# A transformer block on one core: where weight sums are made, and first left sums without PSUM copies

## The chip, the cores and the metric

One Trainium2 chip, one of its cores. The metric is the device time of one execution in microseconds (us). The engines are PE (TensorE, matmuls), PEld (its weight loads), DVE (VectorE), ACT (ScalarE), POOL (GpSimd) and SP (SyncE, which here only issues DMAs). Each engine runs its own instructions in order; an instruction that waits holds up all behind it on its engine.

## The reference

One hybrid decoder block on a sequence of 2048 tokens with 1024 channels, all in float32:

```python
h = _rmsnorm(x, norm_pre_mix)
proj = h @ w_in
y_attn = _mixer_dilated_attention(q, k, v)
y_gmlp = _mixer_chunked_gmlp(u, z, ...)
merged = gate_a * (y_attn @ w_branch_attn) + gate_b * (y_gmlp @ w_branch_gmlp)
x = x + _rmsnorm(merged @ w_out, norm_post_mix)
h = _rmsnorm(x, norm_pre_mlp)
a = relu(h @ w_mlp_in)
x = x + _rmsnorm((a * a) @ w_mlp_out, norm_post_mlp)
```

## The kernel before

**Products.** Each float32 operand is split into a high part of type fp32r (`hi`, a converting copy, mostly on ACT) and the rest (`lo = src - f32(hi)`, a subtraction, mostly on DVE). A product is three matmuls: high by high, high by low, low by high (`mm3`, L98). A 128x512 float32 result fills one of PSUM's eight banks.

**Part 1** makes the projections, the attention and the gate values. The change doesn't touch it.

**Part 2** works on four chunks of 512 tokens, in the order 2, 3, 0, 1. For each, `merge` goes over eight tiles `dt` of 128 channels: two products with the branch weights `wb`, times the gates `g` (loaded by `load_gate` on SP, sigmoid on ACT), summed and split into `mg`. Then four `out_block`s of 128 tokens multiply `mg` by `w_out` (two halves of 24 matmuls), take the norm, add `x` (tile `xr`, one buffer, loaded on SP), store the sum to `x1_d`, and make the normed rows `y1` (L1269). A block's eight transposes (`pt`, L1274) come later on PE: `flush_older` puts those of block 0 in the middle of block 2, those of block 1 in the middle of block 3; the others come in the next merge, or, after the last chunk, in the MLP. `tt` holds the transposed rows on the way to `h2_d`.

`merge` and the blocks also carry *pieces*. The MLP's first product uses a seven-product scheme for 2x2 blocks (Strassen's, in Winograd's form), at two levels, and needs sums of its weights' and its rows' quarters. `w_piece(t)` loads a pair of weight tiles on SP into `trw` and `tqw` (one buffer each), makes four sums on DVE, and stores them with two DMAs on POOL's queue to `ws_d`; `t_piece` does so with rows of `h2_d`. A call of `next_piece` either loads a piece or makes the sums of the one loaded, so a piece needs two calls. `PIECE_AT` says behind which `dt` of which chunk a call stands; one more stands behind each `out_block` of the first three chunks. `W_EARLY` is the number of weight pieces made here; the other of the 16 are made in the MLP.

The order on ACT, DVE, POOL and SP in this part is made by a scheduler. PE's is the written one.

**PSUM in part 2**: four banks for products, and four, with the tag `aux`, that rotate: `junk` (the target of a square), `pt`, and the copies described next. A tile gets the bank of the fourth tile before it in the written order.

**The MLP** has a written order on all engines. Its first half runs 7 x 8 steps of seven products of six matmuls; `k` counts these products. A step needs the *left sums* `hs_n`: raw weights `hraw_n` (two buffers, `load_ha`), of which `combine` makes seven operands: four sums on POOL and three splits of 128x512, `sa`, `sb` and `sc`, made by `staged`. `staged` copies a sum to its high part and a second time to a PSUM bank, both on ACT; DVE later subtracts from that bank. The sets `hs_0` and `hs_1` are made in part 2, before block 2 of the last chunk; these banks are of the tag `aux`, in the order sa, sb, sc, sa, sb, sc, and the two tiles `pt` of block 0 follow them.

`later(k, f, ...)` puts `f` behind product `k`. For the weight sums that part 2 leaves, `w_load` issues four loads, `w_sum` makes one sum each (two on DVE, two on POOL), `w_store` issues four stores.

Of the kernel before, what the change touches and what calls it, by code (L numbers as in the profile page):

```python
# [11 lines left out]
AF = mybir.ActivationFunctionType  # L12
# [8 lines left out]
KT = 8  # L21
# [7 lines left out]
def f32(ap):  # L29
    return ap.bitcast(F32) if ap.dtype != F32 else ap  # L30
# [12 lines left out]
def block_kernel(ctx, tc, a, out):  # L43
    nc = tc.nc
    pe, act, dve, pool, sp = nc.tensor, nc.scalar, nc.vector, nc.gpsimd, nc.sync
    x = a["x"]

    def stack(es, name, bufs=1, side=None, space=None):
        kw = dict(name=name, bufs=bufs, reuse_waits="tile")
        if side:  # L50
            kw["side"] = side
        if space is not None:
            kw["space"] = space
        return es.enter_context(tc.tile_pool(**kw))
# [11 lines left out]
    def psum_aux(name):  # L66
        return ps.tile([P, 512], F32, name=name, tag=aux_tag, bufs=BANKS[aux_tag])

    BANKS, aux_tag = dict(aux=4, a=3, bc=3, s=2), "aux"
# [112 lines left out]
    def behind():  # L182

        es, t = ExitStack(), mybir.EngineType
        for e in (t.Activation, t.DVE, t.Pool, t.SP):
            es.enter_context(tc.issue_after(next(i for i in reversed(nc.cur_bb.bb.instructions) if i.engine == e)))
        return es
# [969 lines left out]
    def load_y(c, engs=(("act", "dve"),)):  # L1157
        cs = slice(c * 512, (c + 1) * 512)
        yt = [bot.tile([P, 2, 512], F32R, name=f"yt{c}{k}", tag=f"yt{k}") for k in range(6)]
        for k in range(6):  # L1160
            split_in(yt[k], ya_d[k, :, cs] if k < 2 else yg_d[k - 2, :, cs], None, *engs[k % len(engs)])
        return yt
# [17 lines left out]
    def load_gate(c, dt, wch):  # L1180
        if dt < KT and (c, dt, wch) not in gates:
            d = chunks.index(c) * KT + dt
            pl, tag = (gtp, f"gt{wch}") if c == 2 or d % (5 - 2 * wch) < 3 - wch else (gxp[0], f"gx{wch}")
            gt = pl.tile([P, 512], F32, name=f"g{wch}_{c}{dt}", tag=tag, bufs=3 - wch if pl is gtp else 2 - wch)
            sp.dma_start(gt, gate_d[wch * 8 + dt, :, c * 512:(c + 1) * 512])
            gates[c, dt, wch] = gt
# [104 lines left out]
    def t_piece(kk):  # L1291

        w, v = (ttp.tile([P, 2, 512], F32, name=f"{n}{kk}", tag=n, bufs=1) for n in ("tq", "tr"))
        for t, k in ((w, kk), (v, kk + 2)):
            sp.dma_start(t.rearrange("p c t -> p (c t)"), h2_d[:, k, HALF:])
        yield
        b11, b12, b21, b22 = w[:, 0], w[:, 1], v[:, 0], v[:, 1]
        dve.tensor_sub(b11, b12, b11)
        dve.tensor_sub(b12, b22, b12)
        pool.dma_start(t_d[:, kk, 0:2], w)  # L1300
        dve.tensor_sub(b22, b22, b11)
        dve.tensor_sub(b21, b21, b22)
        pool.dma_start(t_d[:, kk, 2:4], v)
        yield

    def w_piece(t):

        w, v = (ttp.tile([P, 2, 512], F32, name=f"{n}w{t}", tag=n, bufs=1) for n in ("tq", "tr"))
        for z, n in ((v, t + NF // 2), (w, t)):
            sp.dma_start(z.rearrange("p a c -> p (a c)"), a["w_mlp_in"][n].rearrange("p k c -> p (k c)"))  # L1310
        yield
        a11, a12, a21, a22 = w[:, 0], w[:, 1], v[:, 0], v[:, 1]
        q, f = divmod(t, 2)
        dve.tensor_add(a22, a21, a22)
        dve.tensor_sub(a21, a11, a21)
        pool.dma_start(ws_d[q][:, 2:4, f], v)
        dve.tensor_sub(a11, a22, a11)
        dve.tensor_sub(a12, a12, a11)
        pool.dma_start(ws_d[q][:, 0:2, f], w)
        yield  # L1320

    W_EARLY = 14
    pieces = deque([w_piece(t) for t in range(W_EARLY - 2)] + [t_piece(0), t_piece(1)] +
                   [w_piece(t) for t in range(W_EARLY - 2, W_EARLY)])
    piece = []
    PIECE_AT = {2: (3, 5, 7), 3: (0, 2, 4, 6, 7), 0: (1, 3, 5, 7), 1: range(KT)}

    def next_piece():
        with behind():
            if piece:  # L1330
                next(piece.pop(), None)
            elif pieces:
                piece.append(pieces.popleft())
                next(piece[0])

    def merge_pieces(c, dt):
        if dt in PIECE_AT[c]:
            next_piece()
# [4 lines left out]
    def bank(name, tag):  # L1343
        return ps.tile([P, 512], F32, name=name, tag=tag, bufs=BANKS[tag])
# [2 lines left out]

    def staged(name, src, hi, lo):

        while len(unread) > 1:  # L1350
            unread[0]()
        t = bank(name, "s") if aux_tag != "aux" else psum_aux(name)
        if len(src.shape) == 4:
            t = t.rearrange("p (k m c) -> p k m c", k=2, m=2)
        elif len(src.shape) == 3:
            t = t.rearrange("p (k c) -> p k c", k=2)
        act.activation(hi, src, AF.Copy)  # L1357
        act.activation(t, src, AF.Copy)

        def read():  # L1360
            if read in unread:
                unread.remove(read)
                dve.tensor_sub(lo, t, f32(hi))

        unread.append(read)
        return read
# [56 lines left out]
    def sum_ha(n):  # L1423
        w = hs_[n] = ring(n, f"hs_{n}", [P, 2, 7, 256])
        yield from combine(n, w, hraw_.pop(n))
# [3 lines left out]
    def first_op(j):  # L1429

        name = OPS[j]
        for kk in range(2):
            w = w2_[(0, kk), name] = spot()
            if name[0] == "T":
                src = t_d[:, kk, T_AT.index(name)]
            else:
                k, t0 = kk + 2 * (name[1] == "2"), HALF + 512 * (name[2] == "2")
                src = h2_d[:, k, t0:t0 + 512]
            sp.dma_start(f32(w[1]), src)

    def first_split(j, kk, lo_eng="dve"):
        hi, lo = w2_[(0, kk), OPS[j]]
        split(hi, lo, f32(lo), "act", lo_eng)
# [91 lines left out]
    def w_load(t):  # L1535

        outer_t["w", t] = [rx.tile([P, 512], F32, name=f"wt{t}{m}", tag="xs" if (t - W_EARLY) % 2 else "c1", bufs=4) for m in range(4)]
        for m, z in enumerate(outer_t["w", t]):
# [131 lines left out]
    for n, c in enumerate(chunks):  # L1670
        if n:
            mg = merge(c, yt, {0: flush, 2: flush}, lambda dt: merge_pieces(c, dt))
        for i in range(4):
            b = out_block(c, i, mg, flush_older)
            next(b)
            last.append(b)
            if n < 3:
                next_piece()
            if n < 3 and not i:
                yt = load_y(chunks[n + 1])  # L1680
                for dt, wch in ((0, 0), (0, 1), (1, 0), (1, 1), (2, 0), (2, 1), (3, 0), (4, 0)):
                    with behind():
                        load_gate(chunks[n + 1], dt, wch)
            if n == 3 and i == 1:
                e2r.close()
                egx.close()
                rx = stack(e3, "rx", 1, side="right")
                r4 = stack(e3, "r4", 1, side="right")
                for m in range(4):
                    w = r4.tile([P, 2, 512], F32R, name=f"spot{m}", tag=f"spot{m}")  # L1690
                    spots.append((w[:, 0], w[:, 1]))
                for m in range(2):
                    w = [gtp.tile([P, 512], F32R, name=f"spot{4 + m}{h}", tag=f"gt{m}", bufs=3 - m) for h in range(2)]
                    spots.append(w)
                first_op(0)
                load_ha(0)
                first_op(1)
                load_ha(1)
                first_op(2)
                for g in sum_ha(0):  # L1700
                    pass
                for j in range(2):
                    for kk in range(2):
                        first_split(j, kk)
                for g in sum_ha(1):
                    pass
                for kk in range(2):
                    first_split(2, kk)
# [57 lines left out]
    aux_tag = "bc"  # L1766
# [176 lines left out]
    for n in range(8):  # L1943
        t = 4 + 4 * n
        for f, d, args in ((outer_load, 0, ()), (outer_sum, 4, (0,)), (outer_sum, 6, (2,)), (outer_store, 9, ())):
            later(t + d, f, n, *args)
    for n in range(NF // 2 - W_EARLY):
        t = 38 + 5 * n
        for f, d, args in ((w_load, 0, ()), (w_sum, 4, (0,)), (w_sum, 5, (1,)), (w_sum, 6, (2,)), (w_sum, 7, (3,)),
                           (w_store, 9, ())):  # L1950
            later(t + d, f, W_EARLY + n, *args)
    for q in range(HQ):
        t = 7 * (5 * HQ + 4) + 19 * q // 2
# [4 lines left out]
    for k, (_, stage, n, i) in enumerate(yorder):  # L1958
# [40 lines left out]
        elif i in (3, ("p", 7)):  # L1999
# [10 lines left out]
            if stage and not more:  # L2010
                f = finish(n)
# [73 lines left out]
```

## Time and profile before

| what | value |
|---|---|
| median of 3 runs | 2620.88 us (2618.87 to 2622.3) |
| the profiled execution | 2623.96 us |
| its span, first to last instruction | 2622.3 us |
| mean granted TensorE clock | 0.991 of full |
| PE busy | 2551.4 us, 97% |
| DVE, ACT, POOL busy | 64%, 49%, 52% |
| part 2 | about 1025 to 1437 us |
| first half of the MLP | 1437 to 1993 us |

The span is that of the execution that was profiled, and the time of that execution is a little longer. PE is busy nearly always, so what another engine does shows only where PE waits for it, in a list of who waited for whom (engine, line, releaser; then us in total, times, longest) and in the timeline, where the wait ahead of an instruction stands in square brackets. In the timeline a row is: start, duration, engine, line, operation, output<-inputs, shape. In the groups by line it is: count | busy us, mean ns of one | idle us ahead. In rows by window it is: window and its length, PE, PEld, DVE, ACT, POOL busy (and count), granted clock, DMA share, GB/s.

### The profile page before, as it was taken

Reading aid. Unit: us, or ns where it says so; the run is one execution under the profiler, and the core shown is the slowest. Engines: PE = TensorE matmul, PEld = TensorE weight load, DVE = VectorE, ACT = ScalarE, POOL = GpSimd, SP = SyncE. Lnnn points to the kernel's source line nnn. Section 1 sums busy time; section 2 is a strip of 40 time slices with the busy share of each in tenths; the row PEclk is TensorE's granted clock in tenths of the full one; section 3 lists DMA queues with packets and bytes.
Section 4 is the critical chain, followed back from the end, with each engine's and each line's share of the span. In section 5 each row is a group of like instructions: output and inputs, shape, how many; then the busy total and the mean of one; then the engine's idle time right before and its main releaser. Section 6 shows DMA issues by size and latency. Waiting matters only on the chain. (4 is left out here: it accounts for less than half of the span.)

```text
span 2622.3 us, 36291 instructions
## 1 busy us (share of the span) xinstructions
PE 2551.4 (97%) x12122; PEld 2126.4 (81%) x12122; DVE 1687.3 (64%) x3077; ACT 1294.4 (49%) x2714; POOL 1361.8 (52%) x1377
## 2 busy tenths in 40 slices
PE   9999999999999999999997999999999999999998
PEld 8888888888888887787775778878877888888886
DVE  5676575435443456866665677778776777677767
ACT  5213211244445434554433664675456776666755
POOL 0363254274555544311112656776798677677634
PEclk9999999999999999999998999999999999999999
DMA  8879778989898899866765765347885221222235
GB/s 313 285 246 325 258 235 276 309 261 284 275 312 227 237 305 338 281 242 232 260 226 195 271 196 180 122 145 240 261 270 159 89 89 58 88 89 84 89 117 209
DMA packets 411565, 568.73 MB, mean 217 GB/s; under 512 B 58737, under 2 KB 247409, under 8 KB 410354
## 3 DMA queue, kind: packets, MB, share of 16 engines
q1 hardware_dynamic: 385008, 501.58, 58.8%
q0 software_dynamic: 16480, 58.21, 5.7%
q10 hardware_dynamic: 9890, 6.62, 0.8%
q8 instruction: 96, 1.57, 0.2%
q14 instruction: 91, 0.75, 0.1%
HBM read 362.16 MB, written 204.14 MB: 216 GB/s over the span
## 5 line engine op out<-in xcount | busy, mean ns | idle before, releaser
L1570 PE MATMUL ha<-spot,hs 128*128 128x512 f32 x1344 | 326.6, 391 | 8.7 <-DVE e L1584 2.7
L1880 PE MATMUL ya<-spot,s 128*128 128x512 f32 x1344 | 324.0, 389 | 1.7 <-DVE X_yt L1888 1.4
L1570 PEld LDWEIGHTS ha<-spot,hs 128*128 128x128 f32 x1344 | 252.2, 188 | 65.3 <-DVE e L1584 4.4
L1880 PEld LDWEIGHTS ya<-spot,s 128*128 128x128 f32 x1344 | 252.0, 188 | 55.2 <-DVE X_yt L1888 1.8
L1357 ACT ACTIVATE s<-sraw 128x512 fp32r<-128x512 f32 x168 | 105.3, 627 | 152.5 <-POOL sraw L1409 113.3
L1357 ACT ACTIVATE hs<-hraw 128x512 fp32r<-128x512 f32 x168 | 105.2, 626 | 137.4 <-POOL hraw L1409 108.8
L731 PE MATMUL g<-opA,spots 128*128 128x512 f32 x672 | 170.6, 398 | 1.8 <-DVE cv L763 1.8
L1880 PE MATMUL yc<-spot,s 128*128 128x512 f32 x672 | 170.5, 389 | 0.0
L1570 PE MATMUL hc<-spot,hs 128*128 128x512 f32 x672 | 170.5, 389 | 0.0
L731 PE MATMUL g<-opB,spots 128*128 128x512 f32 x648 | 164.0, 397 | 0.0
L99 PE MATMUL x<-hT_a,wq 128*128 128x512 f32 x384 | 149.7, 390 | 0.0
L100 PE MATMUL x<-hT_a,wq 128*128 128x512 f32 x384 | 149.4, 389 | 0.0
L101 PE MATMUL x<-hT_a,wq 128*128 128x512 f32 x384 | 149.4, 389 | 0.0
L74 ACT ACTIVATE hl<-r 128x512 fp32r<-128x512 f32 x48 | 30.4, 633 | 237.3 <-POOL r L332 89.0
L1570 PEld LDWEIGHTS hc<-spot,hs 128*128 128x128 f32 x672 | 126.1, 188 | 26.3
L1880 PEld LDWEIGHTS yc<-spot,s 128*128 128x128 f32 x672 | 126.1, 188 | 26.2
L731 PEld LDWEIGHTS g<-opA,spots 128*128 128x128 f32 x672 | 121.0, 188 | 23.9 <-issue 2.2
L82 POOL TENSOR_TENSOR spots<-gr,spots 128x512 fp32r<-128x512 f32 x98 | 128.6, 1316 | 21.2 <-ACT spots L74 7.1
L1741 ACT ACTIVATE sraw<-sraw 128x1024 f32<-128x1024 f32 x128 | 134.7, 1053 | 1.7
L731 PEld LDWEIGHTS g<-opB,spots 128*128 128x128 f32 x648 | 116.9, 188 | 21.1
L82 POOL TENSOR_TENSOR spot<-w2r,spot 128x512 fp32r<-128x512 f32 x79 | 101.0, 1306 | 50.2 <-ACT spot L74 50.2
L76 POOL TENSOR_SCALAR spots<-gr 128x512 fp32r<-128x512 f32 x86 | 55.5, 645 | 132.8 <-PE g L731 91.4
(465 smaller groups left out, 6772.9 us busy)
## 6 DMA issues: line engine op xcount, KB each, us to landing
sraw<-sd SPq DMA_DIRECT2D x128, 256.0 KB, 3.3
qk<-hl SPq DMA_DIRECT2D x24, 1024.0 KB, 5.6
qq<-qk SPq DMA_DIRECT2D x96, 256.0 KB, 5.3
sd<-e SPq DMA_DIRECT2D x64, 256.0 KB, 4.6
hraw<-wsd SPq DMA_DIRECT2D x32, 512.0 KB, 4.7
w2r<-in_w_mlp_out_dram SPq DMA_DIRECT2D x16, 1024.0 KB, 8.4
g<-gated SPq DMA_DIRECT2D x56, 256.0 KB, 6.1
gr<-sgd SPq DMA_DIRECT2D x53, 256.0 KB, 5.0
```

The lines of the kernel that those rows point to most:

```text
L74: act.activation(hi, src, AF.Copy)
L76: pool.tensor_scalar(hi, src, 1.0, 1.0, op0=OP.mult, op1=OP.mult)
L82: (pool if lo_eng == "pool" else dve).tensor_sub(lo, src, f32(hi))
L99: pe.matmul(ps, lh, rh, start=start, stop=False)
L100: pe.matmul(ps, lh, rl, start=False, stop=False)
L101: pe.matmul(ps, ll, rh, start=False, stop=stop)
L731: pe.matmul(p, w[:, l, k], h[:, r, k], start=i in (1, 6, 5, 4) and not k and not m, stop=k == 3 and m == 2, skip_group_check=True)
L1357: act.activation(hi, src, AF.Copy)
L1570: pe.matmul(p, w[:, l, S_AT[i], kk * P:(kk + 1) * P], b[r], start=i in (1, 2, 5) and not kk and not z, stop=kk == 1 and z == 2, skip_group ...
L1741: act.activation(sraw_[n], sraw_[n], func)
L1880: pe.matmul(p, s[:, l], w[r], start=i in (1, 2, 5) and not m and not o, stop=m == 1 and o == 2, skip_group_check=True)
```

## The change

It makes 11 weight pieces in part 2 instead of 14, and moves three to the MLP, which now makes five: three in its first phase of 56 products and two in its third, at times from a short table. The calls stand at every second tile `dt`. Behind block 0 of a chunk the call comes after the loads for the next chunk. While the banks `aux` are in use, `staged` makes no copy in PSUM: DVE subtracts from the raw sum in SBUF.

```diff
-    W_EARLY = 14
+    W_EARLY = 11
...
-    PIECE_AT = {2: (3, 5, 7), 3: (0, 2, 4, 6, 7), 0: (1, 3, 5, 7), 1: range(KT)}
+    PIECE_AT = {2: (4, 6), 3: (1, 3, 5, 7), 0: (1, 3, 5, 7), 1: (1, 3, 5, 7)}
...
     def staged(name, src, hi, lo):
+        act.activation(hi, src, AF.Copy)
+        if aux_tag == "aux":
+            return lambda: dve.tensor_sub(lo, src, f32(hi))
         while len(unread) > 1:
             unread[0]()
-        t = bank(name, "s") if aux_tag != "aux" else psum_aux(name)
+        t = bank(name, "s")
...
-        act.activation(hi, src, AF.Copy)
         act.activation(t, src, AF.Copy)
...
-            if n < 3:
-                next_piece()
             if n < 3 and not i:
                 yt = load_y(chunks[n + 1])
...
+            if n < 3:
+                next_piece()
...
     for n in range(NF // 2 - W_EARLY):
-        t = 38 + 5 * n
-        for f, d, args in ((w_load, 0, ()), (w_sum, 4, (0,)), (w_sum, 5, (1,)), (w_sum, 6, (2,)), (w_sum, 7, (3,)),
-                           (w_store, 9, ())):
+        t = (37, 43, 48, 124, 127)[n]
+        for f, d, args in ((w_load, 0, ()), (w_sum, 4, (0,)), (w_sum, 4, (1,)), (w_sum, 5, (2,)), (w_sum, 6, (3,)),
+                           (w_store, 7, ())):
             later(t + d, f, W_EARLY + n, *args)
```

Since a scheduler sets the order in part 2, these lines move more than they name. PE's instructions keep their order. In the rows below, the digits in a name are chunk and block or tile (`y1_10` is block 0 of chunk 1, the last chunk), and a buffer's number comes last.

DVE, at the out blocks of the last chunk, before: all subtractions of `hs_0` and `hs_1` stand behind the last instruction of `y1_11` (and so of `y1_10`).

```order
L1269 SCALAR_TENSOR_TENSOR y1_11_12736<-xr_11_12682,r_pm11_12758,gmlp_10425 128x1024
L1363 TENSOR_TENSOR hs_0_12795<-sa_0_12797,hs_0_12795 128x512
L1363 TENSOR_TENSOR hs_0_12795<-sb_0_12806,hs_0_12795 128x512
L1363 TENSOR_TENSOR hs_0_12795<-sc_0_12810,hs_0_12795 128x512
L82 TENSOR_TENSOR spot2_12779<-spot2_12779 128x512
L82 TENSOR_TENSOR spot3_12780<-spot3_12780 128x512
L1363 TENSOR_TENSOR hs_1_12822<-sa_1_12824,hs_1_12822 128x512
```

DVE there in the changed kernel:

```order
L1352 TENSOR_TENSOR hs_0_12765<-hraw_0_12757,hs_0_12765 128x512
L116 TENSOR_SCALAR t_pm10_12647<-t_pm10_12647 128x1
L1352 TENSOR_TENSOR hs_1_12786<-hraw_1_12761,hs_1_12786 128x512
L117 TENSOR_TENSOR r_pm10_12642<-r_pm10_12642,t_pm10_12647 128x1
L1352 TENSOR_TENSOR hs_1_12786<-hraw_1_12761,hs_1_12786 128x512
L1269 SCALAR_TENSOR_TENSOR y1_10_12620<-xr_10_12566,r_pm10_12642,gmlp_10421 128x1024
```

Five of the six (two more of `hs_0` stand just above) moved ahead of the last instruction of `y1_10`.

SP's queue at the same place, before:

```order
L1310 DMA trw13_12562<-in_w_mlp_in_dram 128x1024
L1310 DMA tqw13_12561<-in_w_mlp_in_dram 128x1024
L1240 DMA xr_11_12682<-in_x_dram 128x1024
L1439 DMA spot0_12777<-h2d_80 128x512
L1439 DMA spot1_12778<-h2d_80 128x512
L1399 DMA hraw_0_12787<-in_w_mlp_in_dram 128x2x512
```

and in the changed kernel (`spot` tiles are right operands of the MLP's first products):

```order
L1310 DMA trw10_12505<-in_w_mlp_in_dram 128x1024
L1310 DMA tqw10_12504<-in_w_mlp_in_dram 128x1024
L1441 DMA spot51_12754<-td_81 128x512
L1441 DMA spot0_12747<-h2d_80 128x512
L1441 DMA spot1_12748<-h2d_80 128x512
L1401 DMA hraw_0_12757<-in_w_mlp_in_dram 128x2x512
```

The load of block 1's `xr` no longer stands ahead of `hraw_0`; it now stands behind `hraw_2`. `spot1` and `hraw_0` take memory that the last weight piece uses, so both wait for its stores.

ACT at the end of the first chunk's merge, before:

```order
L74 ACTIVATE mg24_10297<-g0_25_10055 128x512
L74 ACTIVATE wo6_10008<-woraw6_10256 128x1024
L74 ACTIVATE wo7_10009<-woraw7_10291 128x1024
L74 ACTIVATE yt30_10520<-yt30_10520 128x512
L74 ACTIVATE mg24_10297<-gates3_10085 128x512
```

and in the changed kernel:

```order
L74 ACTIVATE mg24_10293<-g0_25_10055 128x512
L74 ACTIVATE wo6_10008<-woraw6_10256 128x1024
L74 ACTIVATE mg24_10293<-gates3_10085 128x512
L74 ACTIVATE wo7_10009<-woraw7_10291 128x1024
L74 ACTIVATE yt30_10510<-yt30_10510 128x512
```

The high part of tile 6 of `mg` moved ahead of a part of `w_out`, `wo7`, which waits for its own load.

ACT at block 0 of the second chunk, before and then in the changed kernel: the sigmoid of `g0_04` moved ahead of the squares, and two of the three table loads here are gone.

```order
L106 ACT_TABLE_LOAD
L106 ACTIVATE r_post30_11211<-s1_30_11209,edge_95 128x1
L1194 ACT_TABLE_LOAD
L1194 ACTIVATE g0_04_11276<-g0_04_11276 128x512
L1266 ACTIVATE y1_30_11202,s2_30_11221<-xr_30_11148 128x1024
L1259 ACTIVATE junk_310_11333,ss_31_11280<-o_310_11281 128x512
L106 ACT_TABLE_LOAD
L106 ACTIVATE r_pm30_11224<-s2_30_11221,edge_95 128x1
```

```order
L106 ACT_TABLE_LOAD
L106 ACTIVATE r_post30_11201<-s1_30_11199,edge_95 128x1
L1266 ACTIVATE y1_30_11192,s2_30_11211<-xr_30_11138 128x1024
L1259 ACTIVATE junk_310_11323,ss_31_11270<-o_310_11271 128x512
L106 ACTIVATE r_pm30_11214<-s2_30_11211,edge_95 128x1
```

## The prediction

> **What bounds the kernel now.** I read the busy shares first, then who PE waits for, then the stretch around its longest wait engine by engine. The first line of the page says that PE is the bound:
>
> ```profile
> PE 2551.4 (97%) x12122; PEld 2126.4 (81%) x12122; DVE 1687.3 (64%) x3077; ACT 1294.4 (49%) x2714; POOL 1361.8 (52%) x1377
> ```
>
> The change touches no matmul, so it can only move the 70.9 us in which PE is idle (2622.3 - 2551.4), and the matmuls that run slowly. PE's waits, from the list of who waited for whom:
>
> ```profile
> PE pt L1274 <- DVE hs L1363: 18.3, 2, 17.0
> PE pt L1274 <- DVE y L1269: 4.3, 2, 3.0
> PE hb L1570 <- ACT tt L1275: 3.0, 1, 3.0
> ...
> PE o L99 <- ACT mg L74: 2.5, 1, 2.5
> PE o L101 <- DVE mg L82: 2.4, 1, 2.4
> ```
>
> The largest is the one that the edit of `staged` aims at. PE's timeline there:
>
> ```profile
> 1366.41 0.39 PE L99 MATMUL o<-wo,mg 128*128 128x512 f32 x1
> ...
> 1368.45 0.39 PE L99 MATMUL o<-wo,mg 128*128 128x512 f32 x1
> ...
> 1373.46 0.50 PE L101 MATMUL o<-wo,mg 128*128 128x512 f32 x1 [2.35 <-DVE mg L82]
> ...
> 1374.86 0.63 PE L100 MATMUL o<-wo,mg 128*128 128x512 f32 x1
> ...
> 1377.42 0.63 PE L100 MATMUL o<-wo,mg 128*128 128x512 f32 x1
> ...
> 1415.06 1.12 PE L1274 MATMUL pt<-ident,y 128*128 128x128 f32 x4 [17.02 <-DVE hs L1363]
> 1417.44 1.11 PE L1274 MATMUL pt<-ident,y 128*128 128x128 f32 x4 [1.27 <-DVE hs L1363]
> ...
> 1445.61 2.00 PE L1570 MATMUL hb<-spot,hs 128*128 128x512 f32 x5 [2.98 <-ACT tt L1275]
> ```
>
> The nine matmuls from 1366.41 to 1368.45 come 0.227 us apart. At 1374.86 to 1377.42, just after the wait of 2.35, the six steps between are 0.427 us apart; eight matmuls go that way, 8 x 0.2 = 1.6 us. So a wait costs its length and often some 1.6 us of slow matmuls behind it. [...]
>
> Why PE waits 17 us: DVE, ACT, SP and POOL there.
>
> ```profile
> 1395.93 0.69 DVE L1315 TENSOR_TENSOR trw<-tqw,trw 128x512 f32<-128x512 f32 x1 [3.74 <-DMA tqw<-in_w_mlp_in_dram]
> 1399.09 1.28 DVE L1269 SCALAR_TENSOR_TENSOR y<-xr,r_pm,gmlp 128x1024 f32<-128x1024 f32 x1
> 1404.38 1.28 DVE L1264 SCALAR_TENSOR_TENSOR xr<-y,r_post,xr 128x1024 f32<-128x1024 f32 x1 [2.17 <-DMA xr<-in_x_dram]
> 1409.11 1.83 DVE L1269 SCALAR_TENSOR_TENSOR y<-xr,r_pm,gmlp 128x1024 f32<-128x1024 f32 x1
> 1414.31 0.69 DVE L1363 TENSOR_TENSOR hs<-sc,hs 128x512 fp32r<-128x512 f32 x1 [0.91 <-ACT sc L1358]
> 1419.57 0.69 DVE L1363 TENSOR_TENSOR hs<-sb,hs 128x512 fp32r<-128x512 f32 x1 [2.19 <-ACT sb L1358]
> ```
> ```profile
> 1407.83 0.42 ACT L1405 ACTIVATE hs<-hraw 128x256 fp32r<-128x256 f32 x1 [0.28 <-DMA hraw<-in_w_mlp_in_dram]
> ```
> ```profile
> 1367.01 0.32 SPq L1295 DMA_DIRECT2D tr<-h2d  x1
> ...
> 1400.45 0.33 SPq L1240 DMA_DIRECT2D xr<-in_x_dram  x1
> ...
> 1401.87 0.38 SPq L1399 DMA_DIRECT2D hraw<-in_w_mlp_in_dram  x1
> ```
>
> Out block 0 of the last chunk has its normed rows `y1_10` at 1399.09 + 1.28 = 1400.4. But the bank that its transposes want still holds `sc_0`, which DVE reads at 1414.31, and that waited for `hraw_0`: its load stood on SP behind the `xr` load of block 1, which waited for `y1_10`; that waited on DVE behind a weight piece whose load came late (3.74).
>
> **The change, part by part.** PSUM copies: six ACT copies go, and with them the bank. The transposes then wait only for `y1_10`. But the new order puts five of the six subtractions of `hs_0` and `hs_1` ahead of `y1_10`'s last DVE instruction, where before all six stood behind it. So what is late next is that instruction. I follow it, with these rows for the DMAs (KB each, then us from issue to landing):
>
> ```profile
> xr<-in_x_dram SPq DMA_DIRECT2D x16, 512.0 KB, 4.0
> x1d<-xr POOLq DMA_DIRECT2D x16, 512.0 KB, 3.5
> ...
> tqw<-in_w_mlp_in_dram SPq DMA_DIRECT2D x14, 512.0 KB, 6.1
> ...
> wsd<-tqw POOLq DMA_DIRECT2D x14, 512.0 KB, 4.2
> ```
>
> 1. The chunk's last piece, now `w10`, is loaded where the second `t_piece` stood: issued at 1367.0, landed at 1373.1, three further DVE sums of 0.69 to 1375.2, store landed at about 1380. On SP `hraw_0` stands behind a load that waits for this store: issued at about 1380.5, not 1401.87, and no longer behind `xr`.
> 2. In the trace the first ACT instruction on `hraw_0` starts 5.96 us after issue (1401.87 to 1407.83): 1386.5 now. From there to the end of the second set's middle subtraction it took 12.4 us (1407.83 to 1419.57 + 0.69). Fewer copies shorten that, other rows that now stand between (a square, a `junk`, two converts) lengthen it: 10 to 13, then 1.28 for `y1_10`. It ends between 1397.5 and 1400.8; I take 1398.5.
> 3. PE comes to the transposes after five half blocks of 24 matmuls at 0.227: 1366.4 + 27.2 = 1393.6, if the wait of 2.35 and its slow matmuls go, since the late tile's low part no longer stands behind a piece that waits for its load. So PE still waits about 5 us.
> 4. Then the chain from block to block sets the pace: `xr` has one buffer, so each `xr` load waits for the block before.
>
> ```profile
> 1428.56 1.29 DVE L1264 SCALAR_TENSOR_TENSOR xr<-y,r_post,xr 128x1024 f32<-128x1024 f32 x1
> ...
> 1432.23 1.28 DVE L1269 SCALAR_TENSOR_TENSOR y<-xr,r_pm,gmlp 128x1024 f32<-128x1024 f32 x1
> ...
> 1440.37 1.81 DVE L1264 SCALAR_TENSOR_TENSOR xr<-y,r_post,xr 128x1024 f32<-128x1024 f32 x1
> ```
>
> A block takes 4.0 for `xr` and 4.95 (1428.56 to 1433.51) to 6.56 (1404.38 to 1410.94): 9 to 10.6. Two blocks after 1398.5 are 1416.5 to 1419.7, block 3's `xr` lands 4 later, and from its L1264 to PE's first product after the `tt` wait it was 5.24 (1440.37 to 1445.61). That product now starts at 1425.7 to 1428.9, against 1445.61: 16.7 to 19.9 us earlier. The store of `x1` lands in 3.5, inside the 3.7 that the fast case leaves it, so I take nearer the fast end: **-18.5**. This holds the 2.35 and its 1.6 too.
>
> Pieces at every second tile, three fewer in part 2: the six loads on SP, twelve DVE sums of 0.69 and six stores on POOL that go lay beside PE's work and cost it nothing by themselves. What counts are rows that no longer stand behind a late load.
>
> ```profile
> 1111.65 1.06 ACT L74 ACTIVATE wo<-woraw 128x1024 fp32r<-128x1024 f32 x1 [2.18 <-DMA woraw<-in_w_out_dram]
> ...
> 1113.13 0.61 ACT L74 ACTIVATE mg<-gates 128x512 fp32r<-128x512 f32 x1
> ```
> ```profile
> L106 ACT ACT_TABLE_LOAD x11 | 14.1, 1283 | 0.2
> ```
>
> At the end of the first chunk ACT now converts `mg` before that second `wo`, which waits 2.18 for its load: the PE wait of 2.5 goes, with about 1.6 of slow matmuls: **-4.1** (bounds 0 and -4.1; PE asks for this tile just when it is ready, so nearer the latter). In the second chunk two table loads of 1.283 leave the chain that ends in the 3.0 us wait for `y` L1269: **-2.6** (bounds 0 and -3.0). `next_piece` behind `load_y` puts gate loads ahead of piece loads on SP; the waits for gates that this could help I leave at nothing.
>
> The MLP gets three more weight sums, one in the first phase and two in the third.
>
> ```profile
> L1546 POOL TENSOR_TENSOR wt<-wt,wt 128x512 f32<-128x512 f32 x2 | 2.6, 1304 | 1.2 <-DVE wt L1544 1.2
> ...
> L1548 DVE TENSOR_TENSOR wt<-wt,wt 128x512 f32<-128x512 f32 x2 | 1.4, 681 | 0.0
> ```
> ```profile
> 1437.00:1515.00 78.00, 74.17 (x326) 60.43 (x326) 50.87 (x79) 50.57 (x100) 48.90 (x53) 0.98 0.79 273
> ...
> 1592.00:1668.00 76.00, 76.00 (x337) 62.94 (x336) 61.37 (x94) 39.79 (x77) 52.21 (x57) 1.00 0.43 135
> ```
>
> Each is 2 x 0.68 on DVE, 2 x 1.30 on POOL and eight DMA issues on SP. The stores stand on SP seven products after the loads instead of nine, so SP waits there for POOL's last sum, with the next `hraw` load behind it; that load is two steps ahead of its use, 14 products x 6 matmuls x 0.227 = 19 us, which covers it. The sums' cover is POOL's idle time, 29 of 78 us in the first phase and 24 of 76 in the third, and the PSUM banks that PE has in hand. Queued behind them on POOL stand the sums that ACT and DVE convert; without cover one piece costs its 2.6 on POOL, all three 7.8. Below zero it can't go, since nothing is taken away here. PE had no wait in the third phase, so I take **+2**.
>
> Sum: -18.5 - 4.1 - 2.6 + 2 = -23.2. The profiled execution took 2623.96, so 2600.8; the median of the three runs is 3.1 below that: **2598**.
>
> **Rivals.**
> *The subtractions hold DVE longer.* With two SBUF operands instead of one in PSUM they share more with POOL, whose chain feeds them:
>
> ```profile
> 1409.94 1.59 POOL L1409 TENSOR_TENSOR hraw<-hraw 128x256 f32<-128x256 f32 x1
> ```
> ```profile
> L1409 POOL TENSOR_TENSOR hraw<-hraw 128x256 f32<-128x256 f32 x56 | 43.1, 769 | 4.4
> ```
>
> That sum takes 1.59, twice its group's 0.769, where it overlaps the L1269 of 1409.11, itself 1.83 instead of 1.28. If each of five subtractions costs 0.8 so, and the `w10` load comes 4 late, `y1_10` is 8 later: 2606; with a slow `x1` store too, 2611. [...] Chance 0.20.
> *The MLP gives it back.* All 7.8 of POOL and a stage buffer that a late store holds: 8 to 10 more, 2606. Chance 0.09.
> *Slower.* `hraw_0` still lands as late as before. Then `y1_10` comes 12 + 1.3 us after it, 1421, not 1400.4, and PE's wait grows by 6: with -4.1, -2.6 and +2 that is no change. The point from which it decides is a landing at about 1408; at 1416 it is 2629. For it: SP takes its loads in order, and several wait. Against: nothing ahead of `hraw_0` now waits for `y1_10`. Chance 0.04.
> *The wait isn't the copies'.* If another holder of the bank keeps PE, only -4.6 remains: 2616. Against: the subtraction at 1414.31 ends at 1415.00, and the transposes start at 1415.06. Chance 0.04.
>
> **How the numbers follow.** Forecast 0.58 (gain 17 to 32), more than that 0.05. The gain reaches 33 if `y1_10` is ready when PE comes and the MLP costs nothing: 2588. The second rival's end, 2611, is the other end; what lies outside is about 0.15. Some 0.2% (5.2 us) is what a measurement of this kernel can tell from no change: faster are the forecast, the more than that, and the first two rivals, 0.92; the fourth and a quarter of the third lie within, 0.05; the rest of the third is slower, 0.03.
>
> **What would show it.** Right: the 17.02 wait shrinks to 3 to 7 us and names DVE `y`; `hraw_0`'s first ACT instruction comes some 20 us after the chunk's first `o` matmul, not 41; the wait on `tt` before the first `hb` stays at 2 to 7; 2.35 and 2.47 are gone. Wrong: a wait above 12 at those transposes, or PE waits of over 8 us in all that are new in the first and third MLP phases.

## The result, and the profile after

The changed kernel takes 2598.38 us in the median of four runs (2597.95 to 2599.76), the kernel before 2621.56 beside it: a ratio of 0.9914, 95% interval 0.9897 to 0.9932. Run twice more on other occasions it gave 0.9921 (0.9908 to 0.9935) and 0.9920 (0.9907 to 0.9934). The forecast of 2598 holds, but two of its terms were wrong by some 4 to 6 us each, with opposite signs, and its largest term was put down to the wrong part of the change.

The busy line of the page after, and the list of who waited for whom (us in total, times, longest):

```profile
PE 2550.3 (98%) x12122; PEld 2126.4 (82%) x12122; DVE 1687.8 (65%) x3071; ACT 1282.7 (49%) x2702; POOL 1367.1 (53%) x1377
```
```profile
PE b L99 <- DVE g L1211: 4.9, 3, 1.8
PE ha L1572 <- DVE e L1586: 3.6, 3, 2.2
...
PE ha L1572 <- DVE X L1588: 2.3, 1, 2.3
...
PE pt L1274 <- DVE y L1269: 2.0, 1, 2.0
PE ha L1572 <- ACT X_y L1584: 1.5, 1, 1.5
...
PE hb L1572 <- ACT tt L1275: 1.4, 1, 1.4
```

PE idles 45.9 us (2596.2 - 2550.3) instead of 70.9. The wait of 17.0 is gone, and so are 2.5 and 2.35 for `mg` (0.4 is left). New in the MLP are 2.3 for `X` and 0.8 for `X_y`, and a wait of 1.3 for `e` grew to 2.2. The end of part 2 after, in the timelines of PE, SP, ACT and DVE:

```profile
1356.06 0.39 PE L99 MATMUL o<-wo,mg 128*128 128x512 f32 x1
...
1385.42 1.06 PE L1274 MATMUL pt<-ident,y 128*128 128x128 f32 x8 [1.99 <-DVE y L1269]
...
1412.77 1.65 PE L1572 MATMUL hb<-spot,hs 128*128 128x512 f32 x6 [1.38 <-ACT tt L1275]
...
1419.72 1.52 PE L1572 MATMUL hc<-spot,hs 128*128 128x512 f32 x6
```
```profile
1367.95 0.38 SPq L1401 DMA_DIRECT2D hraw<-in_w_mlp_in_dram  x1
```
```profile
1371.60 0.42 ACT L1407 ACTIVATE hs<-hraw 128x256 fp32r<-128x256 f32 x1 [1.12 <-DMA hraw<-in_w_mlp_in_dram]
```
```profile
1372.62 1.24 DVE L1352 TENSOR_TENSOR hs<-hraw,hs 128x512 fp32r<-128x512 f32 x1
...
1383.53 1.75 DVE L1269 SCALAR_TENSOR_TENSOR y<-xr,r_pm,gmlp 128x1024 f32<-128x1024 f32 x1
...
1388.54 1.29 DVE L1264 SCALAR_TENSOR_TENSOR xr<-y,r_post,xr 128x1024 f32<-128x1024 f32 x1 [1.23 <-DMA xr<-in_x_dram]
...
1397.63 1.28 DVE L1264 SCALAR_TENSOR_TENSOR xr<-y,r_post,xr 128x1024 f32<-128x1024 f32 x1 [1.38 <-DMA xr<-in_x_dram]
...
1408.06 1.28 DVE L1264 SCALAR_TENSOR_TENSOR xr<-y,r_post,xr 128x1024 f32<-128x1024 f32 x1
```

`hraw_0` is asked for 11.9 us after the last chunk's first `o` matmul (1367.95 - 1356.06); before it was 35.5 (1401.87 - 1366.41). Its sums are done before PE comes to the transposes, and PE waits 2.0 for the rows themselves.

To see where time goes, the start of one and the same matmul in two traces is compared. Three parts are told apart in all that follows: up to the last chunk's first `o` matmul, from there to the first `hc` product of the MLP, and from there to the end of the span. In the profile of before that `hc` product is this:

```profile
1454.16 1.52 PE L1570 MATMUL hc<-spot,hs 128*128 128x512 f32 x6
```

Against the profile of before, this kernel's parts are -10.4, -24.1 and +8.3: together the -26.1 between the spans (2622.3 and 2596.2).

### The profile page after: what moved, and what is told of

Read it like the earlier page. It is cut to its first block, busy times and chain, and to the rows that moved or that the text cites. A ratio compares the mean times of both kernels' runs of the same rounds, so it can differ in the third digit from the quotient of the medians.

```text
span 2596.2 us, 36297 instructions
## 1 busy us (share of the span) xinstructions
PE 2550.3 (98%) x12122; PEld 2126.4 (82%) x12122; DVE 1687.8 (65%) x3071; ACT 1282.7 (49%) x2702; POOL 1367.1 (53%) x1377
```

## The experiments

Each run is timed in five rounds beside the kernel before. "hraw" is the time from the last chunk's first `o` matmul to the issue of `hraw_0`'s load; the next columns are the second and third part of each profile against the profile of before, in us.

| run | median | ratio (95%) | hraw | last chunk | MLP |
|---|---|---|---|---|---|
| before | 2619 to 2621 | 1 | 35.5 | 0 | 0 |
| copies_only | 2614.7 | 0.9984 (0.9974 to 0.9994) | 31.9 | -10.5 | +1.1 |
| pieces_only | 2602.3 | 0.9935 (0.9923 to 0.9947) | 12.0 | -21.6 | +8.1 |
| last_only | 2606.7 | 0.9946 (0.9933 to 0.9959) | 11.5 | -22.7 | +2.3 |
| last_eight | 2605.1 | 0.9942 (0.9929 to 0.9954) | 32.2 | -11.6 | +2.5 |
| after_again | 2601.5 | 0.9921 (0.9908 to 0.9935) | 11.9 | -24.4 | +7.9 |
| after_third | 2598.8 | 0.9920 (0.9907 to 0.9934) | 10.4 | -25.1 | +6.1 |
| no_move | 2601.5 | 0.9932 (0.9919 to 0.9944) | 11.9 | -24.0 | +9.4 |
| spaced | 2602.8 | 0.9937 (0.9921 to 0.9953) | 9.1 | -25.2 | +10.5 |
| third_raw | 2595.9 | 0.9912 (0.9896 to 0.9928) | 10.2 | -23.5 | +2.6 |
| third_spaced | 2596.9 | 0.9911 (0.9898 to 0.9925) | 10.0 | -25.2 | +3.5 |
| two_first | 2605.1 | 0.9944 (0.9931 to 0.9958) | 11.8 | -23.1 | +12.0 |
| best | 2598.4 | 0.9916 (0.9903 to 0.9929) | 10.1 | -25.8 | +3.0 |

**Copies or pieces?** The first two runs each make one half of the change.

```diff
 copies_only: the kernel before, and in `staged`
+        act.activation(hi, src, AF.Copy)
+        if aux_tag == "aux":
+            return lambda: dve.tensor_sub(lo, src, f32(hi))
         while len(unread) > 1:
             unread[0]()
-        t = bank(name, "s") if aux_tag != "aux" else psum_aux(name)
+        t = bank(name, "s")
...
-        act.activation(hi, src, AF.Copy)
         act.activation(t, src, AF.Copy)
```

> The kernel before with the edit of `staged` alone: its PSUM copies are gone while the tag is aux, all pieces and weight sums stay where they were. Theory A (the PSUM copies held the bank that the last chunk's transposes waited for): the 17.0 us wait shrinks to 2 to 5 us and some 22 us of the stretch from the last chunk's o matmuls to the first hb product go; the 11 us that the changed kernel gains earlier in part 2 stay lost, and the 8.5 us that it gives back in the MLP are not given back: 2597 to 2602 us. Rival B (fewer pieces cleared the queues so that hraw_0 came early; the copies alone are little): gain under 8 us, 2614 us or more, and a wait of over 10 us remains at those transposes.

```diff
 pieces_only: the changed kernel, and in `staged`
-        act.activation(hi, src, AF.Copy)
-        if aux_tag == "aux":
-            return lambda: dve.tensor_sub(lo, src, f32(hi))
         while len(unread) > 1:
             unread[0]()
-        t = bank(name, "s")
+        t = bank(name, "s") if aux_tag != "aux" else psum_aux(name)
...
+        act.activation(hi, src, AF.Copy)
         act.activation(t, src, AF.Copy)
```

> The changed kernel with `staged` as it was before (PSUM copies and their late reads): pieces at every second tile, next_piece behind load_y and five weight sums in the MLP remain. Theory A (copies): the stretch of 22 us is lost again and only the 11 us earlier in part 2 less 8.5 us of the MLP remain: 2616 to 2622 us, with a wait of over 12 us for DVE hs at the transposes. Rival B (pieces): 2600 to 2606 us.

Theory A, the theory of my prediction, falls. The copies alone bring 0.16% (4 us), the pieces' part alone 0.65% (17 us). Rival B has the times right, but not the wait of over 10 us that it left at the transposes. PE in copies_only, then SP and ACT there:

```profile
1395.06 1.06 PE L1274 MATMUL pt<-ident,y 128*128 128x128 f32 x8 [1.31 <-DVE y L1269]
...
1424.09 4.74 PE L1572 MATMUL ha<-spot,hs 128*128 128x512 f32 x12 [8.89 <-ACT junk L1259]
```
```profile
1396.40 0.38 SPq L1401 DMA_DIRECT2D hraw<-in_w_mlp_in_dram  x1
```
```profile
1413.65 0.63 ACT L1350 ACTIVATE hs<-hraw 128x512 fp32r<-128x512 f32 x1 [1.95 <-POOL hraw L1411]
1415.98 0.63 ACT L1350 ACTIVATE hs<-hraw 128x512 fp32r<-128x512 f32 x1 [1.70 <-POOL hraw L1415]
1418.04 0.30 ACT L106 ACTIVATE r_post<-s,edge 128x1 f32<-128x1 f32 x1 [1.43 <-DVE s L1262]
1420.53 1.06 ACT L1266 ACTIVATE y<-xr 128x1024 f32<-128x1024 f32 x1 [2.19 <-DVE xr L1264]
...
1423.33 0.59 ACT L1259 ACTIVATE junk<-o 128x512 f32<-128x512 f32 x1
```

Without the copies the transposes do go at once, with a wait of 1.31. But `hraw_0` is still loaded late, 31.9 after the first `o`, and the conversions of its sums now stand on ACT between one out block's norm and the next. ACT comes to the last `o` bank at 1423.33, and PE, which needs that bank for `ha`, waits 8.9. The wait has moved by two blocks and lost half its length. With the copies in place but fewer pieces, PE's wait at the transposes and two rows of DVE are these (pieces_only):

```profile
1391.97 1.95 PE L1274 MATMUL pt<-ident,y 128*128 128x128 f32 x8 [2.63 <-DVE t_post L116]
```
```profile
1385.89 1.85 DVE L1269 SCALAR_TENSOR_TENSOR y<-xr,r_pm,gmlp 128x1024 f32<-128x1024 f32 x1
...
1391.22 0.69 DVE L1363 TENSOR_TENSOR hs<-sc,hs 128x512 fp32r<-128x512 f32 x1 [0.53 <-ACT sc L1358]
```

The rows `y1_10` are done at 1387.74 (1385.89 + 1.85), but the bank still holds `sc_0` until 1391.91 (1391.22 + 0.69), and PE starts right after that. The releaser named, `t_post`, is a short instruction that ends at the same time. So the copies still hold the bank when `hraw_0` comes early, and PE waits 2.6 us for it. The changed kernel waits 2.0 there instead, since its subtractions stand ahead of `y1_10`.

**Which pieces?** Two runs change the last chunk's pieces alone, from both sides.

```diff
 last_eight: the changed kernel, and
-    W_EARLY = 11
+    W_EARLY = 13
-    PIECE_AT = {2: (4, 6), 3: (1, 3, 5, 7), 0: (1, 3, 5, 7), 1: (1, 3, 5, 7)}
+    PIECE_AT = {2: (4, 6), 3: (1, 3, 5, 7), 0: (1, 3, 5, 7), 1: range(KT)}
```

> The changed kernel with pieces at all eight tiles of the last chunk again (13 weight sums in part 2, three in the MLP, all in its first phase). Theory P (the pieces of the last chunk, whose loads stand ahead of hraw_0 in SP's queue and wait there for a free buffer, are what kept hraw_0 late): hraw_0's load is issued some 15 to 30 us after the chunk's first o matmul instead of 12, PE waits 6 to 9 us before its first products, and with the third phase's 4 to 6 us saved the time is 2602 to 2608 us. Rival Q (the fewer pieces of the earlier chunks are what counts): hraw_0 comes as early as in the changed kernel and only the third phase's saving remains, 2592 to 2595 us.

```diff
 last_only: the kernel before, and
-    W_EARLY = 14
+    W_EARLY = 12
-    PIECE_AT = {2: (3, 5, 7), 3: (0, 2, 4, 6, 7), 0: (1, 3, 5, 7), 1: range(KT)}
+    PIECE_AT = {2: (3, 5, 7), 3: (0, 2, 4, 6, 7), 0: (1, 3, 5, 7), 1: (1, 3, 5, 7)}
-        t = 38 + 5 * n
+        t = (37, 43, 124, 127)[n]
+        # n < 2: sums at +4, +4, +5, +6, store at +7; else +4, +5, +6, +7 and +9
```

> The kernel before, its PSUM copies and its earlier chunks' pieces kept, with pieces at every second tile of the last chunk alone (12 weight sums in part 2, four in the MLP: two in the first phase, two in the third, these at +4, +5, +6, +7). Theory P (the last chunk's pieces alone kept hraw_0 late): hraw_0's load is issued 11 to 14 us after the chunk's first o matmul instead of 35, the 17.0 us wait falls to 2 to 5 us, some 21 us go there and 2 to 4 come back in the MLP: 2601 to 2605 us. Rival Q (the earlier chunks' pieces or the copies decide): hraw_0 stays 25 us or more behind and the time is 2614 us or more.

Theory P holds both ways. Four calls instead of eight in the last chunk, which is two pieces instead of four, take `hraw_0` from 35.5 to 11.5 after the first `o` and 22.7 us out of that stretch; the time was 2606.7, somewhat above what was expected. Eight calls in the changed kernel put it back to 32.2, a little later than expected, and the 8.9 wait with it. One thing these runs do not tell apart: with eight calls the last chunk makes the two `t_piece`s and two weight pieces, with four calls two weight pieces alone, and the `t_piece`s go to the chunk before. So it may be the number of pieces or their kind. SP and DVE in last_eight show what stands ahead of `hraw_0`:

```profile
1366.16 0.33 SPq L1310 DMA_DIRECT2D trw<-in_w_mlp_in_dram  x1
...
1374.63 0.33 SPq L1310 DMA_DIRECT2D trw<-in_w_mlp_in_dram  x1
1376.83 0.33 SPq L1310 DMA_DIRECT2D tqw<-in_w_mlp_in_dram  x1
1385.68 0.33 SPq L1240 DMA_DIRECT2D xr<-in_x_dram  x1
...
1387.09 0.38 SPq L1401 DMA_DIRECT2D hraw<-in_w_mlp_in_dram  x1
```
```profile
1381.16 0.69 DVE L1315 TENSOR_TENSOR trw<-tqw,trw 128x512 f32<-128x512 f32 x1 [2.07 <-DMA tqw<-in_w_mlp_in_dram]
...
1384.32 1.28 DVE L1269 SCALAR_TENSOR_TENSOR y<-xr,r_pm,gmlp 128x1024 f32<-128x1024 f32 x1
```

The last piece's `trw` is asked for at 1374.63 and its `tqw` at 1376.83. DVE waits 2.07 for that load, with `y1_10` behind it, which ends at 1385.60 (1384.32 + 1.28). Block 1's `xr` goes out then, at 1385.68, and `hraw_0` behind it. In the changed kernel the last `trw` and `tqw` go out at 1352.10 and 1355.42.

**The changed kernel again, and the move of `next_piece`.** after_again and after_third are the changed kernel; no_move calls `next_piece` ahead of `load_y`, as before.

> The changed kernel once more, so that the others of this call stand beside it on the same chip. On the chip of the first call the kernel before took 2619.2 us, with the copies back (pieces_only) 2602.3 and without the pieces' part (copies_only) 2614.7. If the copies are worth little beside the pieces, 2597 to 2601 us; by my prediction's account (copies 17 to 20 us) it would be 2585 or less.

> The changed kernel on the chip of this call, to set the other three against: 2597 to 2602 us.

```diff
 no_move: the changed kernel, and in the loop over out blocks
+            if n < 3:
+                next_piece()
             if n < 3 and not i:
                 yt = load_y(chunks[n + 1])
...
-            if n < 3:
-                next_piece()
```

> The changed kernel with next_piece ahead of load_y and the gate loads again. My prediction left this at nothing: 2596 to 2600 us and waits of b for DVE g as before (5 to 8 us in sum). If the gates' place in SP's queue matters, these waits grow by 3 to 8 us: 2601 to 2606 us.

The medians of no_move and after_again are 2601.51 and 2601.48, and the waits of `b` for `g` did not grow (3.4 and 4.5): the move is worth nothing that shows. Beside pieces_only the copies are worth 1 to 4 us (2602.3 against 2598.4 to 2601.5, ratios 0.9935 against 0.9914 to 0.9921), within the intervals, and 2.5 to 3.6 us in the stretch of the last chunk.

**What the MLP gives back.** The five weight sums stand there in two groups, three in the first phase and two in the third.

```diff
 spaced: the changed kernel, and for all five sums
-        ... (w_sum, 4, (0,)), (w_sum, 4, (1,)), (w_sum, 5, (2,)), (w_sum, 6, (3,)), (w_store, 7, ())
+        ... (w_sum, 4, (0,)), (w_sum, 5, (1,)), (w_sum, 6, (2,)), (w_sum, 7, (3,)), (w_store, 9, ())
 third_spaced: the same for the two of the third phase only
 third_raw: the changed kernel, and in `w_sum`
+        if t >= W_EARLY + 3:
+            return
```

> The changed kernel with the four sums of each MLP weight at products +4, +5, +6, +7 and its store at +9, as the kernel before had them, instead of +4, +4, +5, +6 and +7; their number and the times of the loads stay. Theory C (the give-back in the MLP comes from VectorE waiting for GpSimd's sum of the same product, 4.2 us over five sums, with the reads of PE's banks queued behind it): VectorE no longer waits at its second sum, the PE waits of 2.22 and 2.32 go with their slow matmuls, 2592 to 2595 us. Rival D (the work of three more sums costs it wherever it stands): 2597 to 2600 us.

> The changed kernel without the arithmetic of the two weight sums of the third phase (their loads and stores stay; so the weights of the last operator are wrong). If these two sums are what PE's 2.32 us wait and the slow matmuls behind it come from: 4 to 6 us less than the changed kernel, 2592.5 to 2594.5 us. If loads, stores or the queue of SP make that wait: 2597 to 2600 us. The losses of the first phase (1.5, 0.8 and 2.2 us waits around 1482 to 1498 us) stay in both.

> The changed kernel with the two weight sums of the third phase alone at +4, +5, +6, +7 and their store at +9; the three of the first phase stay at +4, +4, +5, +6 and +7, since there the run with all five spaced showed VectorE's e waiting 7.1 us for a late store to free its buffer. Theory C (VectorE waits for GpSimd's sum of the same product): PE's 2.32 us wait of the third phase falls to about 1.2 and its slow matmuls go, 2.5 to 3 us less than the changed kernel, so 2595 to 2597 us, and no wait of 8 us in the first phase. Rival D (the work alone counts): no difference.

The profiles tell these apart better than the times. A phase is 56 products; here it goes from its first product to the first of the next phase, against the profile of before. What the sums of the first phase delay shows at the start of the second, where `e` is made.

| sums in the first and third phase | profiles | second phase | third phase |
|---|---|---|---|
| 2 and none, order of before | copies_only | -0.4 | 0.0 |
| 2 and 2, the latter spaced | last_only, best | +0.4, +0.5 | +1.5 |
| 3 and none | last_eight, third_raw (the third phase's two loaded and stored, but not summed) | +2.0 | 0.0 |
| 3 and 2 | after, after_again, after_third, no_move, pieces_only | +2.0 to +3.6 | +2.6 to +4.2 |
| 3 and 2, the latter spaced | third_spaced | +2.0 | +1.5 |
| 3 and 2, all spaced | spaced | +9.2 | +1.5 |
| 2 and 3 | two_first | +0.5 | +10.1 |

So the two sums of the third phase cost 2.6 to 4.2 us in the changed kernel's order and 1.5 spaced, and the third sum of the first phase costs 1.5 to 3.2 (2.0 to 3.6 against 0.4 to 0.5). The rest of the column MLP isn't the sums': the seventh phase, which no run touches, took up to 1.6 us more than in before (last section). The times don't show it. third_raw and third_spaced are 4.6 to 5.6 us below after_again in the medians, but only 1.5 to 2.5 below the changed kernel's first (2598.4), and all the intervals overlap. Spaced, at 2602.8, is above both ranges that were expected, and third_raw lies between its two. The third phase in the changed kernel, DVE and PE:

```profile
1604.10 1.75 DVE L1550 TENSOR_TENSOR wt<-wt,wt 128x512 f32<-128x512 f32 x1 [1.29 <-POOL wt L1548]
1605.78 0.68 DVE L1365 TENSOR_TENSOR hs<-sb,hs 128x512 fp32r<-128x512 f32 x1
1606.38 0.67 DVE L1588 TENSOR_TENSOR X<-X,ha 128x512 f32<-128x512 f32 x1
```
```profile
1607.11 1.86 PE L1572 MATMUL ha<-spot,hs 128*128 128x512 f32 x6 [2.32 <-DVE X L1588]
1608.76 2.77 PE L1572 MATMUL hc<-spot,hs 128*128 128x512 f32 x6
```

and in third_spaced:

```profile
1609.16 0.67 DVE L1588 TENSOR_TENSOR X<-X,ha 128x512 f32<-128x512 f32 x1
1612.42 0.69 DVE L1550 TENSOR_TENSOR wt<-wt,wt 128x512 f32<-128x512 f32 x1 [2.59 <-POOL wt L1548]
```
```profile
1617.02 3.00 PE L1572 MATMUL ha<-spot,hs 128*128 128x512 f32 x12 [1.19 <-DVE X L1588]
```

Theory C is right on the place and wrong on the reason. DVE waits for POOL's sum as much as ever, 2.59 there. What changed is what stands behind that wait: in the changed kernel it is `X<-X,ha`, which empties a PSUM bank that PE wants; in third_spaced this read is done before. And the sum itself takes 0.69 instead of 1.75: in the changed kernel POOL makes a sum of `hb` beside it (1604.03 to 1605.31), in third_spaced POOL has nothing to do from 1612.39 to 1613.20.

Spacing the first phase's sums too is a loss. In spaced PE waits 8.47 there, because DVE waits:

```profile
1510.65 2.93 PE L1572 MATMUL ha<-spot,hs 128*128 128x512 f32 x6 [8.47 <-DVE e L1586]
```
```profile
1509.91 0.69 DVE L1586 TENSOR_TENSOR e<-X_yt,ha 128x512 f32<-128x512 f32 x1 [7.10 <-DMA wsd<-wt]
```

`e` of the second phase takes the buffer of a `wt` tile whose store, two products later than in the changed kernel, went out only at 1504.82, behind a load of `hb` at 1504.40. Two last runs look for a better split.

```diff
 two_first: the changed kernel, and
-        t = (37, 43, 48, 124, 127)[n]
+        t = (37, 43, 123, 126, 132)[n]
+        # n = 2, 3: sums at +4, +5, +6, +7, store at +9; the others as they were
```

> The changed kernel with two weight sums in the first MLP phase and three in the third (loads at products 37, 43, 123, 126 and 132; the first two of the third phase at +4, +5, +6, +7 and +9). If the third sum of the first phase is what its waits of 1.5, 0.8 and 2.2 us come from, two of these three go and the third phase has room for it: 2593 to 2596 us. If those waits belong to the phase and not to that sum, they stay and the third phase loses 1 to 2 more: 2597 to 2600 us.

best is last_only with the changed kernel's `staged` and place of `next_piece`.

> The changed kernel with the pieces of the first three chunks as before (12 weight sums in part 2), so that four remain for the MLP: two in its first phase, two in the third, these at +4, +5, +6, +7 and their store at +9. If the earlier chunks' pieces hide as well as I think, hraw_0 comes as early as in the changed kernel and the MLP loses 4 to 6 us less: 2593 to 2597 us. If the earlier chunks' pieces are worth the 11 us that the changed kernel's profile shows there: 2602 to 2606 us.

For neither run did one of the expected ranges hold. two_first gives back 12.0: the waits of 0.8 and 2.2 became one of 1.8, but the fifth sum's load went out only at 1609.11, behind the store at 1605.83 that frees its buffer, and DVE waited for that load, with `X<-X,ha` behind it:

```profile
1617.21 0.69 DVE L1546 TENSOR_TENSOR wt<-wt,wt 128x512 f32<-128x512 f32 x1 [6.28 <-DMA wt<-in_w_mlp_in_dram]
1617.82 0.68 DVE L1588 TENSOR_TENSOR X<-X,ha 128x512 f32<-128x512 f32 x1
```

best gives back only 3.0, yet its time is that of after_third (2598.4 and 2598.8): it still has the wait for `mg` at the end of the first chunk (2.9) and most of that for `y` in the second (2.2), which the changed kernel's pieces removed. No run is shown to beat the changed kernel.

## Why the prediction was right, and where it was not

**The end of part 2, -18.5.** Measured -24.1, -24.4 and -25.1 to the first `hc`. To the product behind the wait on `tt`, where my sum ended, it is -22.5, -22.8 and -23.5; up to `hc` another 1.6 goes, since the matmuls behind that wait ran slowly before (8.55 us to `hc`) and don't here (6.95). The chain was the one described. Its issue of `hraw_0` was 2.2 us earlier than I put it (11.9 after the first `o`, not 14.1), and the first ACT instruction came 3.65 after the issue and not 5.96, another 2.3. From that ACT instruction to the end of `y1_10` it took 13.7 (1371.60 to 1385.28), where I took 12.0 of a possible 11.3 to 14.3. So `y1_10` came 2.9 earlier than I put it. The `xr` of later blocks came 9.1 and 10.4 apart (9 to 10.6). The wait at the transposes was 2.0, under the 3 to 7 that I gave, and the wait on `tt` 1.38, under 2 to 7 (2.64 in after_again and after_third).

**Its cause.** The step that failed is the sentence "six ACT copies go, and with them the bank", under which the whole term stood. The earlier load was in my working as step 1, and that step alone does it: last_only keeps the copies and gains 22.7 there. The copies alone gain 10.5 in that stretch, and 2.5 to 3.6 where the load is early. The two halves remove the same wait, so their shares don't add: -10.5 and -21.6 alone, -24 together. I had not asked what each half does by itself. My rival of a late `hraw_0` is what copies_only and last_eight show, at another price: PE's wait at the transposes did not grow, since the scheduler left the subtractions behind `y1_10` there; the bank of `ha` took it over with 8.9.

**The end of the first chunk, -4.1, and the second chunk, -2.6.** Both hold, the second a little past its bound of -3.0. Over the first, from the chunk's first `o` to its third half block, the profiles with the new pieces give -3.6 to -4.7, copies_only -1.1, and best and last_only, whose first chunk has the old pieces, give +0.4 and +2.2. In the second, from the fifth half block to the sixth, between which the transposes of block 0 stand, it is -3.2 in every profile with the new pieces, -0.2 in copies_only and last_only and -0.8 in best. Both come from the pieces.

**The MLP, +2.** This term was mis-sized. The second and third phases together, which are what the sums cost, measured +4.8 to +7.8 in the five profiles, inside my bounds of 7.8 but two to four times the +2; with the other phases the whole gave back 6.1 to 9.4. I counted POOL's and DVE's instructions against their idle time. What they cost is not that time but the place of a DVE instruction that waits for POOL ahead of one that empties PE's bank. That PE had no wait in the third phase before was no cover: with the two sums one of 2.32 came, and in third_raw, which leaves them out, there is none. My windows were also not quite the phases: the first phase of before goes from 1437.5 to 1523.4 and the third from 1601.3 to 1677.5, but POOL's idle time there, 30 and 24 us, is what I took.

**Ahead of the last chunk.** The profile shows -10.4 where my two terms make -6.7. One stretch that I left at nothing agrees in sign everywhere: the third chunk's merge, from the second chunk's last `o` to the third's first, took 42.4 us in before and in copies_only and 34.7 to 39.7 in every other profile, so this too comes from the pieces. The merges of the second and the last chunk give part of it back, by amounts that differ between executions of the same code: -1.8 to +4.8 and +0.2 to +5.5 against before.

So 5.6 us more were gained at the end of part 2 than I had reckoned and 4 to 7 more given back in the MLP, and that the time came out within a microsecond was luck. Of the rivals, the subtractions did last longer, 1.24 and 1.16 at worst, both beside sums on POOL, where the 392 of before that read PSUM (L1363) took 0.694 at most; but all six together took 5.2 where 4.1 was the least (6 x 0.69): 1 us, with 0.5 more for `y1_10` itself (1.75 instead of 1.28), not 4. The rival of the MLP stood at 10 to 12 in all (8 to 10 more than my +2); the measured give-back lies between it and mine, and part 2 gained more than either had.

## What to carry to other kernels

When an engine waits for a buffer, ask first why its holder is late: here the bank's holder was late by its load, and the load by the queue of other loads ahead of it (asked for 35.5 us after the first `o`, and 11.9 with that queue shorter). Two parts of a change that touch one wait must be priced each alone and both together. An instruction that waits for another engine costs what stands behind it on its own engine, so put the reads that empty PE's banks ahead of it: PE waited 2.32 in the third phase with such a read behind it, and 1.19 with the read ahead.

## What the runs showed of the hardware

The same wait of 2.32 us in the third phase is followed by six matmuls in 2.77 us in the profile above, and by six at full pace in after_again, the same kernel:

```profile
1606.87 1.65 PE L1572 MATMUL ha<-spot,hs 128*128 128x512 f32 x6 [2.32 <-DVE X L1588]
1608.36 1.52 PE L1572 MATMUL hc<-spot,hs 128*128 128x512 f32 x6
```

It is so at the transposes too. Behind a wait of 1.99 the `o` matmuls of the changed kernel's profile come 0.43 us apart (seven steps from 1386.55 to 1389.54); behind one of 1.98 in after_again they come 0.23 apart. A wait of 2.5 in the seventh and last phase of the MLP's first half stands in every profile. Here it is before and then in the changed kernel, and the six matmuls behind it take 1.65 and 2.88:

```profile
1918.11 1.65 PE L1570 MATMUL ha<-spot,hs 128*128 128x512 f32 x6 [2.48 <-DVE X_yt L1586]
```
```profile
1891.62 2.88 PE L1572 MATMUL ha<-spot,hs 128*128 128x512 f32 x6 [2.48 <-DVE X_yt L1588]
```

So "a wait and 1.6 us of slow matmuls" holds in some executions only; my sum took it as certain in two places. What decides it no run shows: slow matmuls followed waits of 1.99 and 2.32 in one execution of the changed kernel, and none followed waits of 1.98 and 2.32 in another.

Up to the last chunk's first `o`, where after_again, after_third, spaced, third_raw, third_spaced and two_first run the same code as the changed kernel, the seven profiles stand -10.6 to 0.0 us against before. The waits of `b` for `g`, which hang on gate loads (ACT waited 49.0 us for them in the changed kernel, 29 times), make part of it: 4.9 us in the changed kernel's profile, and in third_raw

```profile
PE b L99 <- DVE g L1211: 8.3, 3, 3.5
```

A single profile says little on a term of this part below 5 us; what is said above of its terms rests on stretches that agree in all profiles.
